# Picking the chosen pairs' expert numbers: thresholds and sums of index differences in place of a one-hot over 50 candidates

## The chip, the cores and the metric

The kernel runs on one core of one Trainium2 chip. The metric is the device time of one execution in microseconds (us). The engines are named PE (TensorE, matmul), DVE (VectorE), ACT (ScalarE), POOL (GpSimd) and SP (SyncE, which issues the transfers here).

## What is computed

Two transformer blocks, one after the other, on 256 tokens of width 1024. The first block ends in a PEER layer: each of 8 heads scores two sets of 128 keys, keeps the 16 best of each, adds them to 16 x 16 pair scores, keeps the 16 best pairs, and the pair's two key numbers name one of 128 x 128 experts. In the reference, cut to what matters here (`ub` and `vb` are the rows of `u` and `v` of the chosen experts, `gb` their gates):

```python
s = jnp.einsum('thpc,hpnc->thpn', q, subkeys).astype(jnp.float32)
s_top, i_top = lax.top_k(s, PEER_TOPK)
cand = s_top[:, :, 0, :, None] + s_top[:, :, 1, None, :]
cand_idx = i_top[:, :, 0, :, None] * PEER_N_KEYS + i_top[:, :, 1, None, :]
best, pos = lax.top_k(cand.reshape(T, PEER_HEADS, PEER_TOPK * PEER_TOPK), PEER_TOPK)
experts = jnp.take_along_axis(cand_idx.reshape(T, PEER_HEADS, PEER_TOPK * PEER_TOPK), pos, axis=-1)
gates = jax.nn.softmax(best, axis=-1).astype(h.dtype)
...
act = jax.nn.gelu(jnp.einsum('cd,ced->ce', xb, ub), approximate=False) * gb
return jnp.einsum('ce,ced->cd', act, vb)
```

The kernel doesn't gather: it computes all 16384 experts' products with the tokens and multiplies them by a gate that is zero for experts not chosen.

## The kernel before, in words

**Weights.** All large weights come as one stream of 128 x 128 blocks, 16 to a transfer (`raw`). `Stream.tile` splits eight blocks at a time into a high and a low part: `whi` is a copy by ACT (`L229`), `wlo` a difference (`L231`) that DVE makes for two tiles in three and POOL for the third (`W.pat = "DDP"`). Both have three buffers (`WB`), and `block` asks for one tile ahead of the one in use. Every product is three matmuls, lines 254 (high weights), 255 (high weights, low part of the tokens) and 256 (low weights).

**The stage around the change.** `both(uphase(0, 64), chain(topk(0), topk(1), topk_fin(0), topk_fin(1)), TKR)` (line 902) writes out the order by hand: after each weight tile of `uphase` (24 matmuls), the generator of the other side is advanced TKR times on average, up to its next `yield`. After every second tile ACT applies a GELU (`L198`, output `as`). `topk(tt)` treats 128 tokens: `top16` finds the 16 best of 128 scores for 16 half-heads (lines 809 to 813, one `yield` each); the sums of the 50 pairs that can be among the 16 best go to `cv` (DVE) and their expert numbers to `ce` (POOL) in seven steps (line 838); `top16` finds the 16 best of the 50 for each of 8 heads (`best`, `pos`, one `yield` each). Then the one-hot: for each head, `eq` (line 854, DVE) compares 16 positions with 50 numbers, `hit` (line 858, POOL) multiplies the result by `ce`, and `ex` (line 862, DVE) adds up over the 50. `eq` and `hit` have two buffers each. Casts, a shift and a mask (lines 869 to 873) make the two key numbers `f1` and `f2`. The softmax of `best` follows. `topk_fin` transposes `f1`, `f2` and the gate on PE (line 894) and copies them to float16 (`i1T`, `i2T`, `gT`).

`pace(r)` puts an instruction behind the last `wlo` that DVE had been given, so that the planner doesn't place it earlier.

**What follows.** `uphase(64, 96)` runs beside `gates(0)`, which builds one-hot matrices `p` and `eq` (lines 919, 921), the products `q` (924), multiplies them on PE (929) and scales the GELU's output `as` by the result (934), all but the matmul on DVE. Later stages: the products with `v`, a second block with convolution, delta rule, window attention and two feed-forward layers.

Of the kernel before, what the change touches and what calls it, by code (L numbers as in the profile page):

```python
# [23 lines left out]
F32 = mybir.dt.float32  # L24
F32R = mybir.dt.float32r
F16 = mybir.dt.float16
BF16 = mybir.dt.bfloat16
U32 = mybir.dt.uint32
AF = mybir.ActivationFunctionType
OP = mybir.AluOpType  # L30
AX = mybir.AxisListType
# [10 lines left out]
FF = 22  # L42
GB = 16
SPLIT_OUT1, SPLIT_XO, SPLIT_MIX, SPLIT_SWA = (3, 7), (3, 4, 6), (3, 4), (2, 5)
LAG, MIXR, TKR, DLR = 2, 1.15, 1.65, 4
EXPAT = "DDP"
NNOP = 0
PAT_QK, PAT_QKV = "DP", "DPP"
LB = 3, 3, 4, 3, 4, 2
# [17 lines left out]
def _consts():  # L67
    i = np.arange(128)
    f = np.float32
    out, at = {}, {}  # L70
    out["ident"] = np.eye(128, dtype=f)
    out["ones"] = np.ones((128, 128), f)
    out["bd64"] = (i[:, None] // 64 == i[None, :] // 64).astype(f)
    c1, out = out, {}
    out["negones"] = -np.ones((128, 128), f)
    out["negu"] = -(i[:, None] >= i[None, :]).astype(f)
    for n, mk in (("mbig", np.where(i[:, None] > i[None, :], f(BIG), f(0))),
                  ("mstr", np.where(i[:, None] >= i[None, :], f(-BIG), f(0)))):
        out[n] = np.concatenate([mk, np.zeros((128, 128), f), mk], 1)
    s4 = np.zeros((128, 4, 128), f)  # L80
    for h in range(4):
        s4[h, h, :] = 1
    out["sel4"] = s4.reshape(128, 512)
    o4 = np.zeros((128, 4, 4), f)
    for h in range(4):
        o4[:, h, h] = 1
    out["onec4"] = o4.reshape(128, 16)
    cm, out = out, c1
    out["eps"] = np.full((128, 1), EPS, f)
    out["iota"] = np.broadcast_to(i.astype(f)[None], (128, 128)).copy()  # L90
    c2 = {}
    hs = np.zeros((128, 2), f)
    hs[:64, 0] = 1
    hs[64:, 1] = 1
    c2["hsel"] = hs
    c2["tri"] = (i[:, None] <= i[None, :]).astype(f)
    c2["after"] = (i[:, None] > i[None, :]).astype(f)
    lv = []
    for s in (1, 2, 4, 8, 16, 32, 64):
        j, q = i[:, None], i[None, :]  # L100
        lv.append(((j // (2 * s) == q // (2 * s)) & ((q & s) > 0) & ((j & s) == 0)).astype(f))
    c2["lev"] = np.concatenate(lv, 1)
    q = np.arange(NMETA, T2)
    k = np.arange(T2)
    vis = (k[None] <= q[:, None]) & ((k[None] < NMETA) | (q[:, None] - k[None] < 128))
    msk = np.where(vis, f(0), f(-BIG)).astype(f)
    c2["msk0"] = msk[:128, :144]
    c2["msk1"] = msk[128:]
    mm = np.zeros((128, NMETA), f)
    mm[0, 15] = -BIG  # L110
    c2["mskm"] = mm

    def pack(d):
        at, o = {}, 0
        for n, a in d.items():
            at[n] = (o, a.shape[1])
            o += a.shape[1]
        return np.concatenate(list(d.values()), 1).astype(f), at

    a1, at1 = pack(c1)  # L120
    am, atm = pack(cm)
    a2, at2 = pack(c2)
    return a1, at1, am, atm, a2, at2
# [17 lines left out]
def tile_two_blocks(ctx, tc, ws, xT, memT, metaT, par_d, wsm_d, subk_d, c1_d, cm_d, c2_d, out, dumps=None):  # L141
    nc = tc.nc
    dumps = dumps or {}
    V, G, A, PE = nc.vector, nc.gpsimd, nc.scalar, nc.tensor

    def dump(name, ap, dst=None):
        if name in dumps:
            d = dumps[name]
            nc.sync.dma_start(d if dst is None else dst(d), ap)
# [23 lines left out]
    def C1(n, p=128):  # L173
        o, w = AT1[n]
        return c1[:p, o:o + w]
# [68 lines left out]
    W = Stream()  # L244
# [497 lines left out]
    with tc.tile_pool(name="pe", bufs=1) as mp:  # L742

        def asub():
            return mp.tile([128, 32, T1], F32, name="as", bufs=3)
# [4 lines left out]
        gT = mp.tile([128, 2, T1], F16, name="gT")  # L750
        iom = mp.tile([128, 128, 8], F16, name="iom")
        V.tensor_copy(iom, C1("iota").unsqueeze(2).to_broadcast([128, 128, 8]))
        iota = C1("iota")
        a0 = asub().rearrange("p a b -> p (a b)")
        subk = a0[:, :2048].rearrange("p (a b) -> p a b", a=16)
        nc.sync.dma_start(subk, subk_d)
# [45 lines left out]
        with tc.tile_pool(name="tk", bufs=1) as tp:  # L802
            def pace(r):

                after(r, W.last)
# [8 lines left out]
            PAIRS = [(a, 1, 16 // (a + 1)) for a in range(5)] + [(5, 3, 2), (8, 8, 1)]  # L814
            NCAND = 50

            fin = {}

            def topk(tt):
                top = tp.tile([128, 16, 16], F32, name="top")  # L820
                idx = tp.tile([128, 16, 16], U32, name="idx")
                for hp in range(16):
                    top16(top[:, hp], idx[:, hp], sc[:, tt, hp], 128)
                    yield
                idf = tp.tile([128, 16, 16], F32, name="idf")
                V.tensor_copy(idf, idx)
                tv = top.rearrange("p (h z) k -> p h z k", z=2)
                iv = idf.rearrange("p (h z) k -> p h z k", z=2)
                V.tensor_scalar(iv[:, :, 0], iv[:, :, 0], 128.0, None, op0=OP.mult)
                cv = tp.tile([128, 8, NCAND], F32, name="cv")  # L830
                ce = tp.tile([128, 8, NCAND], F32, name="ce")
                o = 0
                for a, na, nb in PAIRS:
                    for e, dst, src in ((V, cv, tv), (G, ce, iv)):
                        d = dst[:, :, o:o + na * nb].rearrange("p h (a b) -> p h a b", a=na)
                        x = src[:, :, 0, a:a + na].unsqueeze(3).to_broadcast([128, 8, na, nb])
                        y = src[:, :, 1, :nb].unsqueeze(2).to_broadcast([128, 8, na, nb])
                        e.tensor_add(d, x, y)
                    o += na * nb
                    yield  # L840
                best = tp.tile([128, 8, 16], F32, name="best")
                pos = tp.tile([128, 8, 16], U32, name="pos")
                for h in range(8):
                    top16(best[:, h], pos[:, h], cv[:, h], NCAND)
                    yield
                psf = tp.tile([128, 8, 16], F16, name="psf")
                V.tensor_copy(psf, pos)
                ex = tp.tile([128, 8, 16], F32, name="ex")
                W.pat = EXPAT
                hits = {}  # L850
                for h in range(9):
                    if h < 8:
                        eq = tp.tile([128, NCAND, 2, 8], F16, name="eq", bufs=2)
                        pace(V.tensor_tensor(eq, psf[:, h].rearrange("p (a b) -> p a b", a=2).unsqueeze(1).to_broadcast(
                            [128, NCAND, 2, 8]), iom[:, :NCAND].unsqueeze(2).to_broadcast([128, NCAND, 2, 8]),
                            op=OP.is_equal))
                        hits[h] = tp.tile([128, 16, NCAND], F32, name="hit", bufs=2)
                        G.tensor_mul(hits[h], eq.rearrange("p c a b -> p (a b) c"),
                                     ce[:, h].unsqueeze(1).to_broadcast([128, 16, NCAND]))
                        yield  # L860
                    if h:
                        pace(V.reduce_sum(ex[:, h - 1], hits.pop(h - 1), axis=AX.X))
                        yield
                W.pat = "DDP"
                eu = tp.tile([128, 128], U32, name="eu")
                i1 = tp.tile([128, 128], U32, name="i1")
                f1 = tp.tile([128, 128], F32, name="f1", bufs=2)
                f2 = tp.tile([128, 128], F32, name="f2", bufs=2)
                V.tensor_copy(eu, ex.rearrange("p h k -> p (h k)"))
                V.tensor_scalar(i1, eu, 7, None, op0=OP.logical_shift_right)  # L870
                V.tensor_copy(f1, i1)
                V.tensor_scalar(i1, eu, 127, None, op0=OP.bitwise_and)
                V.tensor_copy(f2, i1)
                dump("f1", f1, lambda d: d[tt])
                dump("f2", f2, lambda d: d[tt])
                yield
                g = tp.tile([128, 8, 16], F32, name="gt", bufs=2)
                V.tensor_sub(g, best, best[:, :, 0:1].to_broadcast([128, 8, 16]))
                act(g, g, AF.Exp)
                gs = tp.tile([128, 16], F32, name="gs")  # L880
                V.reduce_sum(gs[:, :8], g, axis=AX.X)
                V.reciprocal(gs[:, 8:], gs[:, :8])
                V.tensor_scalar(gs[:, 8:], gs[:, 8:], GSCALE, None, op0=OP.mult)
                V.tensor_mul(g, g, gs[:, 8:].unsqueeze(2).to_broadcast([128, 8, 16]))
                dump("gt", g, lambda d: d[tt].rearrange("p (a b) -> p a b", a=8))
                yield
                fin[tt] = f1, f2, g
# [16 lines left out]
        with tc.tile_pool(name="pg", bufs=1) as tp:  # L904
# [50 lines left out]
            for m in range(KC):  # L955
                V.scalar_tensor_tensor(X1[:, m], ys[m // 2][:, (m % 2) * T1:(m % 2 + 1) * T1], 1.0 / GSCALE, X1[:, m],
                                       op0=OP.mult, op1=OP.add)
# [3 lines left out]
    with tc.tile_pool(name="b2", bufs=1) as bp:  # L961
# [52 lines left out]
        with tc.tile_pool(name="m0", bufs=1) as mp:  # L1014
# [97 lines left out]
            for i, (t0, t1) in enumerate(TT2):  # L1112
                n = t1 - t0
# [226 lines left out]
        with tc.tile_pool(name="m1", bufs=1) as mp:  # L1340
# [197 lines left out]
            ge = early()  # L1538
# [119 lines left out]
```

## Time and profile before

| | us |
|---|---|
| median of 3 timed runs | 1960.94 |
| lowest and highest | 1957.55, 1965.3 |
| the profiled execution | 1955.38 |
| its span, from the first to the last instruction | 1953.7 |
| PE busy in the span | 1843.0 |
| DVE busy | 1361.0 |
| ACT busy | 864.5 |
| POOL busy | 628.8 |

The profile is one execution. A busy share is a mean over stages with different limits, so the stage that holds the change is to be read by itself: by stretches, by what PE waited for, and by the distance of events that mark equal amounts of its work. Durations in the trace are those of single instructions; where two engines wait for each other inside an instruction, the wait is part of its duration.

### The profile page before, as it was taken

To read this page: it belongs to the slowest core of one execution; us is meant where nothing else is said; L and a number is where in the kernel's file an instruction comes from. 1 tells how busy PE (TensorE), PEld (TensorE's weight loads), DVE (VectorE), ACT (ScalarE), POOL (GpSimd) and SP (SyncE) were. 2 spreads that over 40 slices of the span, in tenths; PEclk is the share of its full clock that TensorE was granted. 3 is DMA by queue.
4 is the path that set the end of the run, shared out by engine and by line. 5 is a ranking of instruction groups with operands and counts; after the bars stand their busy time and mean duration, and the time that the engine had idled before them with its cause. 6 is when DMAs were issued, how large, how long until landed. Compare 5 with 4: busy or idle time off the path is not lost.

```text
span 1953.7 us, 36962 instructions
## 1 busy us (share of the span) xinstructions
PE 1843.0 (94%) x15387; PEld 1772.1 (91%) x15387; DVE 1361.0 (70%) x2454; ACT 864.5 (44%) x1343; POOL 628.8 (32%) x384
## 2 busy tenths in 40 slices
PE   7999999989888899998899998899999999989999
PEld 6988999989888799998799998889999999679999
DVE  7746666898999965339974456864778845657872
ACT  5456554434432244443234444332444445644442
POOL 4312322373722222222222223332234422014442
PEclk9999999999999999999999998999999999989999
DMA  6432435535433355553345554211244443124453
GB/s 226 169 109 97 162 109 176 191 130 194 151 131 130 109 174 195 192 183 121 112 149 184 184 194 147 87 65 66 108 148 174 176 174 131 64 87 155 174 190 130
DMA packets 43128, 285.58 MB, mean 146 GB/s; under 512 B 5712, under 2 KB 8528, under 8 KB 9040
## 3 DMA queue, kind: packets, MB, share of 16 engines
q1 hardware_dynamic: 42960, 283.21, 40.7%
q8 instruction: 121, 1.98, 0.4%
q14 instruction: 47, 0.39, 0.1%
HBM read 282.14 MB, written 1.05 MB: 145 GB/s over the span
## 4 chain that ended last, share of the span: by engine, by line
PE 49%; DVE 19%; issue 3%; ACT 1%; POOL 0%; POOLq 0%; DVEq 0%; ACTq 0%
PE ps L254 9%; PE ps L255 9%; PE ps L256 9%; PE y L254 5%; PE y L256 5%; PE y L255 5%; DVE wlo L231 4%; DVE p L919 3%; DVE q L924 3%; DVE as L934 2%; DVE cy L973 2%; DVE eq L921 1%; PE pa L1443 1%; DVE hl L406 1%; DVE cy L971 1%
## 5 line engine op out<-in xcount | busy, mean ns | idle before, releaser
L229 ACT ACTIVATE whi<-raw 128x1024 fp32r<-128x1024 f32 x527 | 557.0, 1058 | 769.5 <-PE ps L255 500.5
L231 POOL TENSOR_TENSOR wlo<-raw,whi 128x1024 fp32r<-128x1024 f32 x180 | 455.6, 2531 | 955.9 <-ACT whi L229 939.7
L256 PE MATMUL ps<-xnh,wlo 128*128 128x256 f32 (+2 forms) x2336 | 677.5, 290 | 25.1 <-POOL wlo L231 15.9
L254 PE MATMUL ps<-xnh,whi 128*128 128x256 f32 (+2 forms) x2336 | 679.8, 291 | 14.1 <-ACT whi L225 6.9
L255 PE MATMUL ps<-xnl,whi 128*128 128x256 f32 (+2 forms) x2336 | 674.9, 289 | 0.8 <-DVE xnl L334 0.8
L231 DVE TENSOR_TENSOR wlo<-raw,whi 128x1024 fp32r<-128x1024 f32 x347 | 453.6, 1307 | 265.1 <-ACT whi L229 263.3
L256 PEld LDWEIGHTS ps<-xnh,wlo 128*128 128x128 f32 x2336 | 452.8, 194 | 31.8 <-POOL wlo L231 17.6
L254 PEld LDWEIGHTS ps<-xnh,whi 128*128 128x128 f32 x2336 | 453.5, 194 | 17.5 <-ACT whi L229 7.3
L255 PEld LDWEIGHTS ps<-xnl,whi 128*128 128x128 f32 x2336 | 451.9, 193 | 3.0 <-issue 1.6
L255 PE MATMUL y<-hl,whi 128*128 128x256 f32 x1024 | 289.8, 283 | 6.4 <-DVE hl L406 6.4
L254 PE MATMUL y<-hh,whi 128*128 128x256 f32 x1024 | 291.7, 285 | 0.5 <-ACT hh L405 0.5
L256 PE MATMUL y<-hh,wlo 128*128 128x256 f32 x1024 | 289.2, 282 | 3.2 <-DVE wlo L231 3.2
L255 PEld LDWEIGHTS y<-hl,whi 128*128 128x128 f32 x1024 | 195.6, 191 | 7.6 <-DVE hl L406 7.6
L256 PEld LDWEIGHTS y<-hh,wlo 128*128 128x128 f32 x1024 | 198.2, 194 | 4.0 <-DVE wlo L231 4.0
L254 PEld LDWEIGHTS y<-hh,whi 128*128 128x128 f32 x1024 | 195.6, 191 | 0.7 <-ACT hh L405 0.7
L406 DVE TENSOR_TENSOR hl<-as,hh 128x512 fp32r<-128x512 f32 x64 | 78.2, 1223 | 34.1 <-ACT hh L405 34.1
L254 PE MATMUL ps<-fh,whi 128*128 128x272 f32 (+1 forms) x352 | 100.1, 285 | 0.0
L256 PE MATMUL ps<-fh,wlo 128*128 128x272 f32 (+1 forms) x352 | 100.1, 284 | 0.0
L255 PE MATMUL ps<-fl,whi 128*128 128x272 f32 (+1 forms) x352 | 100.0, 284 | 0.0
L973 DVE SCALAR_TENSOR_TENSOR cy<-xpad,par,cy 128x272 f32<-128x272 f32 (+1 forms) x132 | 90.7, 695 | 2.6
L919 DVE TENSOR_TENSOR p<-iom,i1T 128x1024 f16<-128x1024 f16 x64 | 75.0, 1172 | 0.0
L929 PE MATMUL pa<-q,p 128*128 128x64 f16 x1024 | 43.5, 195 | 30.8 <-DVE as L934 25.2
(526 smaller groups left out, 2773.4 us busy)
## 6 DMA issues: line engine op xcount, KB each, us to landing
raw<-in_ws_dram SPq DMA_DIRECT2D x263, 1024.0 KB, 4.8
X<-in_xT_dram SPq DMA_DIRECT2D x4, 256.0 KB, 4.3
memX<-in_memT_dram SPq DMA_DIRECT2D x1, 1024.0 KB, 13.1
as<-in_subk_d_dram SPq DMA_DIRECT2D x1, 1024.0 KB, 6.9
out_dram<-X SPq DMA_DIRECT2D x4, 256.0 KB, 2.6
c<-in_c_d_dram SPq DMA_DIRECT2D x1, 793.0 KB, 4.3
cm<-in_cm_d_dram SPq DMA_DIRECT2D x1, 776.0 KB, 11.0
raw<-in_ws_dram SPq DMA_DIRECT2D x4, 128.0 KB, 4.1
```

The lines of the kernel that those rows point to most:

```text
L229: A.activation(hi, s, AF.Copy)
L231: r = e.tensor_sub(lo, s, hi.bitcast(F32))
L254: PE.matmul(ps, wh, xh, start=start, stop=False, **k)
L255: PE.matmul(ps, wh, xl, start=False, stop=False, **k)
L256: PE.matmul(ps, wl, xh, start=False, stop=stop, **k)
L406: V.tensor_sub(lo, x, hi.bitcast(F32))
L919: V.tensor_tensor(p1, index(0, 128), pairs(i1T, 128), op=OP.is_equal)
L921: V.tensor_tensor(eq, index(R * r, R), pairs(i2T, R), op=OP.is_equal)
L924: V.tensor_mul(q[:, z], eq, pairs(gT[:, z], R))
L929: PE.matmul(pg[:, t * R:(t + 1) * R], p1[:, a, :, b], q[:, z, a, :, b], start=z == 0, stop=z == 1)
L934: V.tensor_mul(a, a, pv[:, 32 * s:32 * s + 32])
L973: V.scalar_tensor_tensor(dst, xpad[:, j:j + T], P(wname, o + j), dst, op0=OP.mult, op1=OP.add)
```

## The change

The product with a one-hot over 50 candidates is replaced. The candidates lie in order of their first rank: rank 0 has 16, rank 1 has 8, and so on, so the first rank of a position follows from 16 thresholds, and the second is the position less the last threshold reached. `ge` compares the 16 positions of all 8 heads with the 16 thresholds in one instruction; the sum over ranks of `ge` times the step of the thresholds gives the last threshold reached; the sum of `ge` times the differences of neighbouring first key numbers (`d1`) gives the first key number; a comparison of the remaining rank with 0 to 15, times the second key numbers (`d2`), gives the second. All are float16, on DVE, over 128 x 2048 elements; the sums over 16 ranks are halved by additions (`fold`). `ce`, `hit`, `ex`, the cast to an integer, the shift and the mask go. Two constants of 16 columns are added. TKR goes from 1.65 to 1.5; EXPAT, equal to the pattern in use anyway, goes.

```diff
-LAG, MIXR, TKR, DLR = 2, 1.15, 1.65, 4
-EXPAT = "DDP"
+LAG, MIXR, TKR, DLR = 2, 1.15, 1.5, 4
...
+    thr = np.concatenate([[0], np.cumsum([16 // (a + 1) for a in range(15)])]).astype(f)
+    out["thr"] = np.broadcast_to(thr[None], (128, 16)).copy()
+    out["dthr"] = np.broadcast_to(np.diff(thr, prepend=f(0))[None], (128, 16)).copy()
...
+            thr, dthr, rank = (tp.tile([128, 16, 16], F16, name=n) for n in ("thr", "dthr", "rank"))
+            for t, c in ((thr, C1("thr")), (dthr, C1("dthr")), (rank, C1("iota")[:, :16])):
+                V.tensor_copy(t, c.unsqueeze(2).to_broadcast([128, 16, 16]))
...
-                idf = tp.tile([128, 16, 16], F32, name="idf")
-                V.tensor_copy(idf, idx)
+                iv = idx.rearrange("p (h z) k -> p h z k", z=2)
+                ix = tp.tile([128, 2, 8, 16], F16, name="ix")
+                V.tensor_copy(ix, iv.rearrange("p h z k -> p z h k"))
+                d1 = tp.tile([128, 8, 16, 2], F16, name="d1")
+                d2 = tp.tile([128, 8, 16, 2], F16, name="d2")
+                V.tensor_copy(d1[:, :, 0], ix[:, 0, :, :1].to_broadcast([128, 8, 2]))
+                for e in range(2):
+                    V.tensor_sub(d1[:, :, 1:, e], ix[:, 0, :, 1:], ix[:, 0, :, :15])
+                V.tensor_copy(d2, ix[:, 1].unsqueeze(3).to_broadcast([128, 8, 16, 2]))
+                yield
...
-                    for e, dst, src in ((V, cv, tv), (G, ce, iv)):
...
-                ex = tp.tile([128, 8, 16], F32, name="ex")
-                W.pat = EXPAT
-                hits = {}
-                for h in range(9):
-                    if h < 8:
-                        eq = tp.tile([128, NCAND, 2, 8], F16, name="eq", bufs=2)
-                        pace(V.tensor_tensor(eq, psf[:, h].rearrange("p (a b) -> p a b", a=2).unsqueeze(1).to_broadcast(
-                            [128, NCAND, 2, 8]), iom[:, :NCAND].unsqueeze(2).to_broadcast([128, NCAND, 2, 8]),
-                            op=OP.is_equal))
-                        hits[h] = tp.tile([128, 16, NCAND], F32, name="hit", bufs=2)
-                        G.tensor_mul(hits[h], eq.rearrange("p c a b -> p (a b) c"),
-                                     ce[:, h].unsqueeze(1).to_broadcast([128, 16, NCAND]))
-                        yield
-                    if h:
-                        pace(V.reduce_sum(ex[:, h - 1], hits.pop(h - 1), axis=AX.X))
-                        yield
...
+                def weighted(x, mask, d):
+
+                    pace(V.tensor_mul(x.rearrange("p h j (s e) -> p (h j) s e", e=2),
+                                      mask.rearrange("p h j (s e) -> p (h j) s e", e=2),
+                                      d.rearrange("p h j e -> p (h j) e").unsqueeze(2).to_broadcast([128, 128, 8, 2])))
+
+                def fold(x, out):
+
+                    n = 8
+                    while n > 1:
+                        V.tensor_add(x[:, :, :n], x[:, :, :n], x[:, :, n:2 * n])
+                        n //= 2
+                        if n == 4:
+                            yield
+                    V.tensor_add(out, x[:, :, 0], x[:, :, 1])
+                    yield
+
+                ge, x = cells("ge"), cells("gx")
+                pace(V.tensor_tensor(ge, slots16(psf), over_h(thr), op=OP.is_ge))
+                yield
+                pace(V.tensor_mul(x, ge, over_h(dthr)))
+                yield
+                rb_ = tp.tile([128, 8, 16], F16, name="rb_")
+                yield from fold(x, rb_)
+                V.tensor_sub(rb_, psf, rb_)
+                weighted(x, ge, d1)
+                yield
+                yield from fold(x, f1.rearrange("p (h k) -> p h k", h=8))
+                pace(V.tensor_tensor(ge, slots16(rb_), over_h(rank), op=OP.is_equal))
+                yield
+                weighted(x, ge, d2)
+                yield
+                yield from fold(x, f2.rearrange("p (h k) -> p h k", h=8))
```

## Rows read from the trace of the kernel before

**Rows 1.** The page, part 1: busy us, share of the span, instructions.

```profile
PE 1843.0 (94%) x15387; PEld 1772.1 (91%) x15387; DVE 1361.0 (70%) x2454; ACT 864.5 (44%) x1343; POOL 628.8 (32%) x384
```

**Rows 2.** Stretches: length, PE, PEld, DVE, ACT, POOL busy, granted clock, DMA, GB/s.

```profile
410.00:415.00 5.00, 3.23 (x26) 2.90 (x24) 5.00 (x5) 2.41 (x3) 4.07 (x2) 1.00 0.00 0
...
425.00:430.00 5.00, 0.48 (x2) 0.48 (x3) 5.00 (x3) 1.07 (x2) 4.47 (x2) 0.89 0.02 8
...
510.00:515.00 5.00, 1.68 (x8) 1.69 (x9) 5.00 (x4) 0.00 (x0) 4.43 (x2) 0.59 0.16 26
```

**Rows 3.** What PE waited for from 345 to 545: us, times, longest.

```profile
PE ps L256 <- POOL wlo L231: 12.8, 4, 5.4
```

**Rows 4.** ACT in order of time: start, us, what, idle before.

```profile
398.50 1.06 ACT L229 ACTIVATE whi<-raw 128x1024 fp32r<-128x1024 f32 x1 [1.83 <-PE ps L255]
...
404.13 1.06 ACT L229 ACTIVATE whi<-raw 128x1024 fp32r<-128x1024 f32 x1 [1.78 <-PE ps L255]
...
410.78 0.58 ACT L198 ACTIVATE as<-ps 128x512 f32<-128x512 f32 x1
...
418.89 1.06 ACT L229 ACTIVATE whi<-raw 128x1024 fp32r<-128x1024 f32 x1 [4.69 <-PE ps L255]
419.86 0.58 ACT L198 ACTIVATE as<-ps 128x512 f32<-128x512 f32 x1
...
425.49 0.58 ACT L198 ACTIVATE as<-ps 128x512 f32<-128x512 f32 x1
...
437.37 0.58 ACT L198 ACTIVATE as<-ps 128x512 f32<-128x512 f32 x1
...
505.53 0.58 ACT L198 ACTIVATE as<-ps 128x512 f32<-128x512 f32 x1
...
519.06 0.58 ACT L198 ACTIVATE as<-ps 128x512 f32<-128x512 f32 x1
```

**Rows 5.** POOL in order of time.

```profile
399.64 2.44 POOL L231 TENSOR_TENSOR wlo<-raw,whi 128x1024 fp32r<-128x1024 f32 x1 [6.11 <-ACT whi L229]
402.86 3.35 POOL L858 TENSOR_TENSOR hit<-eq,ce 128x800 f32<-128x800 f16 x1 [0.77 <-DVE eq L854]
...
423.86 2.32 POOL L858 TENSOR_TENSOR hit<-eq,ce 128x800 f32<-128x800 f16 x1 [0.58 <-DVE eq L854]
426.13 3.34 POOL L231 TENSOR_TENSOR wlo<-raw,whi 128x1024 fp32r<-128x1024 f32 x1
```

**Rows 6.** Tiles `eq` and `p`: shortest, median, longest in ns, times of the first and last.

```profile
L924 DVE TENSOR_TENSOR q<-eq,gT x128: 398/415/2577, 545.1 to 997.9; 128x512 f16<-128x512 f16 x128
...
L854 DVE TENSOR_TENSOR eq<-psf,iom x16: 562/1943/2820, 402.2 to 524.9; 128x800 f16<-128x800 f16 x16
...
L919 DVE TENSOR_TENSOR p<-iom,i1T x64: 1042/1074/3195, 541.5 to 993.4; 128x1024 f16<-128x1024 f16 x64
```

**Rows 7.** DVE in order of time.

```profile
396.71 1.23 DVE L231 TENSOR_TENSOR wlo<-raw,whi 128x1024 fp32r<-128x1024 f32 x1 [0.44 <-ACT whi L229]
...
403.83 2.82 DVE L854 TENSOR_TENSOR eq<-psf,iom 128x800 f16<-128x800 f16 x1
```

**Rows 8.** DVE's groups from 345 to 545: busy us, mean ns, idle before.

```profile
L854 DVE TENSOR_TENSOR eq<-psf,iom 128x800 f16<-128x800 f16 x16 | 27.9, 1750 | 0.1
L862 DVE TENSOR_REDUCE ex<-hit 128x16 f32<-128x800 f32 x16 | 15.6, 975 | 3.1 <-POOL hit L858 3.1
...
L869 DVE CAST eu<-ex 128x128 uint32<-128x128 f32 x2 | 2.8, 1388 | 0.1
...
L847 DVE CAST psf<-pos 128x128 f16<-128x128 uint32 x2 | 2.6, 1323 | 0.0
```

**Rows 9.** PE in order of time: the transposes of `topk_fin`.

```profile
538.26 0.38 PE L894 MATMUL pa<-c,f 128*128 128x128 f32 x2
```

**Rows 10.** What PE waited for from 545 to 706: us, times, longest.

```profile
PE pa L929 <- DVE as L934: 18.5, 11, 4.1
```

More of the change, by code (lines that the diff above doesn't have):

```diff
@@ L752, in tile_two_blocks @@
         V.tensor_copy(iom, C1("iota").unsqueeze(2).to_broadcast([128, 128, 8]))
-        iota = C1("iota")
         a0 = asub().rearrange("p a b -> p (a b)")
@@ L824, in topk @@
                     yield
-                idf = tp.tile([128, 16, 16], F32, name="idf")
-                V.tensor_copy(idf, idx)
+                iv = idx.rearrange("p (h z) k -> p h z k", z=2)
[8 more added lines that the diff above has]
+                yield
                 tv = top.rearrange("p (h z) k -> p h z k", z=2)
-                iv = idf.rearrange("p (h z) k -> p h z k", z=2)
-                V.tensor_scalar(iv[:, :, 0], iv[:, :, 0], 128.0, None, op0=OP.mult)
                 cv = tp.tile([128, 8, NCAND], F32, name="cv")
-                ce = tp.tile([128, 8, NCAND], F32, name="ce")
                 o = 0
                 for a, na, nb in PAIRS:
-                    for e, dst, src in ((V, cv, tv), (G, ce, iv)):
[L835 to L838, printed above, removed]
+                    V.tensor_add(cv[:, :, o:o + na * nb].rearrange("p h (a b) -> p h a b", a=na),
+                                 tv[:, :, 0, a:a + na].unsqueeze(3).to_broadcast([128, 8, na, nb]),
+                                 tv[:, :, 1, :nb].unsqueeze(2).to_broadcast([128, 8, na, nb]))
                     o += na * nb
@@ L864, in topk @@
-                W.pat = "DDP"
-                eu = tp.tile([128, 128], U32, name="eu")
-                i1 = tp.tile([128, 128], U32, name="i1")
                 f1 = tp.tile([128, 128], F32, name="f1", bufs=2)
                 f2 = tp.tile([128, 128], F32, name="f2", bufs=2)
[L869 to L872, printed above, removed]
@@ L873, in topk, with cells, over_h, slots16 @@
-                V.tensor_copy(f2, i1)
+                def cells(name):
+                    return tp.tile([128, 8, 16, 16], F16, name=name)
+                def over_h(c):
+                    return c.unsqueeze(1).to_broadcast([128, 8, 16, 16])
+                def slots16(x):
+                    return x.unsqueeze(2).to_broadcast([128, 8, 16, 16])
+                def weighted(x, mask, d):
+                    pace(V.tensor_mul(x.rearrange("p h j (s e) -> p (h j) s e", e=2),
+                                      mask.rearrange("p h j (s e) -> p (h j) s e", e=2),
+                                      d.rearrange("p h j e -> p (h j) e").unsqueeze(2).to_broadcast([128, 128, 8, 2])))
```

## The prediction

> **What bounds the kernel now.** I read the page's busy shares first: TensorE (PE) is busy for 94% of the span and VectorE (DVE) for 70% [rows 1], so a change on DVE counts only where PE waits for DVE or for something queued behind it. The changed lines lie in the stage that runs `uphase(0, 64)` beside `topk`, from about 347 to 543 us. Cut into stretches of 5 us, this stage has PE full nearly everywhere; the worst of the exceptions are 410-415, 425-430 and 510-515, in which the present one-hot runs and PE is busy for 3.23, 0.48 and 1.68 of 5 us [rows 2]. The waits of PE in the stage say on whom: 12.8 us in 4 waits, all of them for a `wlo` tile that GpSimd (POOL) makes, the longest 5.4 us [rows 3]. DVE is not named, though it is full there.
>
> What the stage loses is read best from the GELU that ends every second weight tile (`L198`). Two tiles take 5.65 us where nothing is amiss (419.86 to 425.49, and `whi` from 398.50 to 404.13, are 5.63). Three intervals are longer: 410.78 to 419.86 is 9.08, 425.49 to 437.37 is 11.88, 505.53 to 519.06 is 13.53 [rows 4]. Less 5.65 each, 3.4 + 6.2 + 7.9 = **17.5 us** are lost. That is more than the waits, since the granted clock falls with the long ones (0.59 of full speed in 510-515 [rows 2], so part of it at the lower level, 1.2 GHz, after PE had stood still).
>
> The cause is POOL's queue. Every third tile is POOL's; the one whose `whi` was copied at 418.89 gets its `wlo` only from 426.13, behind the `hit` of 423.86 (2.32 us), which itself had to wait for an `eq` [rows 4, 5]. An undisturbed `wlo` on POOL takes 2.44; this one took 3.34 [rows 5]. DVE suffers in turn: an `eq` of 0.56 us at its shortest took 2.82 from 403.83, and POOL's `hit` ran from 402.86 for 3.35, to 406.21 [rows 5 to 7]. So two-input work on the two engines waits for each other.
>
> The Trainium skill, SBUF — State Buffer, § "SBUF: two separate sides", calls this an exclusive lock: a DVE instruction with two SBUF inputs and a GpSimd instruction exclude each other, and the first to start keeps the pair to its end. The rows agree (2.82 beside 0.56). The rule speaks against the change as well as for it, since the new products are two-input too and will meet POOL's `wlo`; by it each meeting costs one whole instruction. The same figure comes out of the rows below.
>
> **Removed.** On POOL, 16 `hit` (2.32 and 3.35 us in the two rows shown, [rows 5]) and 14 short `ce` sums; POOL keeps only its `wlo`. On DVE, 16 `eq` (27.9 us), 16 `ex` (15.6) and the cast `eu` (2.8): 46.3 us in the stage, half per `topk` [rows 8]. The shorter casts beside them are left out. PE's three losses are all on a `wlo` behind a `hit`; with POOL's queue free, the 17.5 us should go. How much margin a POOL `wlo` then has: `whi` at 398.50 feeds the `wlo` at 399.64, which ends at 402.08; the buffers turn over every third tile, so that the tile is wanted when the `whi` two further on may start, at 404.13 [rows 4, 5]. That leaves 2.05 us. A DVE `wlo` takes 1.23 [rows 7], 1.2 less, so it has 3.3.
>
> **Added.** Per `topk` five float16 instructions of 2048 elements (`is_ge`, a product, two weighted products, `is_equal`), three folds of 1024 + 512 + 256 additions and a last one of 128, and one difference. None is in the trace. The nearest rows are `q` (512 elements, 0.398 at its shortest, pairs broadcast as in `weighted`) and `eq` (800, 0.562) [rows 6]: (0.562 - 0.398) / 288 = 0.57 ns per element and 0.106 fixed. So 1.27, 0.69, 0.40 and 0.25 for 2048, 1024, 512 and 256, and I take 0.25 for the last sum. Sum: 5 x 1.27 + 3 x 1.59 + 0.18 = 11.3 us per `topk`, 22.6 in all against 46.3. From above, `p` (1024 elements, strided, 1.042 [rows 6]) gives 1.98 for 2048, and float32 `wlo` (1024 in 1.23 [rows 7]) gives 2.3. I take the low end, as the new operands are dense or paired like those of `eq` and `q`. Below that nothing in the trace goes.
>
> The Trainium skill, VectorE: DVE Perf Modes, § "The perf-mode tier table", gives 1224 ns for a 16-bit two-tensor operation of 2048 elements and 2293 for a float32 one. By its figure the products would sum to 6.1 instead of 6.4 us, an estimate from that page; no run here shows it yet.
>
> **Does DVE keep up?** The section has 11 yields per `topk`, and TKR 1.5 hands out 4.5 per three tiles, so it lasts 7.3 tiles. Three tiles of PE are 1.5 x 5.65 = 8.5 us. DVE needs 4.5 x 11.3/11 = 4.6, two `wlo` of 1.23, and, at worst, one whole POOL `wlo` of 2.44 spent waiting: 9.5. The excess of 1.0 grows to 2.4 us over 7.3 tiles, below the 3.3 of margin: no stall. POOL's `wlo` waits for at most one DVE product, 1.27, below its 2.05. So the cost is 0 at best; I put **2 us** in for unlucky orders, and the upper end stands with the rivals.
>
> **The hand-over.** Before, `topk` has 49 yields, with the two `topk_fin` 100 in all, and at 1.65 per tile both `topk_fin` fall behind tile 61: their transposes stand together behind that tile, the first at 538.26 [rows 9]. After, it has 45 yields, 92 in all, and at 1.5 the last falls behind tile 62 (61 x 1.5 = 91.5). The `gates` behind it are bound by DVE (PE waits 18.5 us for `as` there [rows 10]), so a start one tile later costs between 0, if DVE does its `wlo` meanwhile, and 2.8. I take **1.5**.
>
> **Edits with one answer.** Index copies, differences and their pairs (`ix`, `d1`, `d2`; five short instructions, at most the 0.415 of a 512-element `q` each [rows 6], some 2 us per `topk`) are hidden by PE's full queue and by TKR: the 16-key part hands out 1.5 yields per tile for 1.65, which gives a tenth of its time back. Without that cover it is 4 us; a cast like `psf`, 1.32 on average [rows 8] for a size that needs far less, can also meet a POOL `wlo`. Three constant copies fall before the first `topk` step, ahead of the first `max`, and have the margin of a `wlo` as cover; uncovered they cost 1. The constants grow by 32 columns, on a transfer at the start that is long over. EXPAT equalled the other pattern, so its removal is nothing. The sum: -17.5 + 2 + 1.5 = **-14 us**. The profiled execution (1955.38 us, span 1953.7) would come to 1941.4; the three timed runs lie higher, at 1957.55 to 1965.3, and from their median of 1960.94 the forecast is **1947 us**.
>
> **Rivals.** *Half the gain:* the new products run at the pace of `p`. Then a `topk` needs 5 x 1.98 + 3 x 2.2 + 0.18 = 16.7 us, 6.8 per three tiles, 11.7 with `wlo` and one meeting, 3.2 too much; over 7.3 tiles 7.8, less the margin 4.5 of stall, 9 for both. -17.5 + 9 + 1.5 = -7: 1954. For it: the strided `p` row, and that no addition in float16 is shown. Against: `q` and `eq`.
>
> *Slower:* they run at the pace of float32 `wlo`: 19.1 us per `topk`, 1.74 per yield, 12.7 per three tiles, 10.2 too much, 6.9 of stall, 14 for both; a 2.3 us product holds POOL's `wlo` beyond its 2.05 (1.5 in all); two long stalls bring the clock down again (6.2 lost at 425 us where PE stood 4.5 [rows 2, 4], so 1.7 each, 3.4); the hand-over costs 2.8. Together 21.7 against 17.5: +4, 1965. It decides from about 1.7 us per yield. Against it: float16 instructions of both kinds of operand are faster in every row of theirs that met no one.
>
> *Absorbed:* DVE, full from 545 on, sets the end of `gates`, and an earlier PE only waits longer: 1961. Against: DVE's part of `gates` starts from `topk_fin`, whose transposes PE does between its tiles [rows 9], so DVE's start moves with PE.
>
> **How the numbers follow.** Forecast 0.62 (1943 to 1951 by its terms, some microseconds more by the spread of the runs), half the gain 0.22, absorbed 0.06, slower 0.10. The range of 8 in 10 goes from 1940 to 1961. A measurement of this kernel can tell about 0.5%, 9.8 us, from no change. Faster by more: 0.62; within: 0.31 (half, absorbed, and a slow rival that stays small); slower by more: 0.07.
>
> **What would show it.** Right: the three long GELU intervals fall to about 5.7; PE's waits for POOL's `wlo` in the stage fall below 3 us; products of 2048 elements take 1.2 to 1.3 us where POOL is idle and up to 3.7 where it isn't; the `gates` stretch keeps its length. Wrong: products near 2 us, PE waits for DVE's `wlo` in the new section, or a `gates` stretch longer by what the stage gained.

## The result, and the profile after

| | before | after |
|---|---|---|
| median of the timed runs, us | 1959.24 (4 runs) | 1941.64 (4 runs) |
| lowest and highest | 1957.28, 1965.30 | 1937.70, 1945.23 |
| ratio with 95% interval | | 0.9887 (0.9852 to 0.9922) |
| profiled execution, its span | 1955.38, 1953.7 | 1937.70, 1936.0 |

By that ratio the changed kernel is 1.1% faster. On the 1960.94 us that the prediction started from, the ratio is 1938.8 us (1931.9 to 1945.6 over the interval): the sign and the place were forecast, the size was not. 1947 lies above the interval, and 1938.8 lies 1.2 below the low end of 1940. The quotient of the two medians shown is 0.9910 (17.6 us); it lies inside the interval too, so that a few microseconds are within what these runs can tell. From profile to profile the span fell by 17.7 us.

The page's first part for the changed kernel answers to [rows 1] (busy us, share of the span, instructions):

```profile
PE 1844.8 (95%) x15387; PEld 1773.0 (92%) x15387; DVE 1335.9 (69%) x2457; ACT 865.8 (45%) x1343; POOL 574.9 (30%) x354
```

DVE is busy for 25.1 us less and POOL for 53.9 less, while PE is busy as before: it has less idle time. The three stretches of [rows 2], in the changed kernel (length, PE, PEld, DVE, ACT, POOL busy, granted clock, DMA share, GB/s):

```profile
410.00:415.00 5.00, 5.00 (x45) 5.00 (x44) 4.93 (x4) 2.61 (x3) 1.72 (x1) 1.00 0.45 138
425.00:430.00 5.00, 5.00 (x45) 5.00 (x44) 4.90 (x5) 3.25 (x5) 3.38 (x1) 1.00 0.59 205
510.00:515.00 5.00, 5.00 (x45) 5.00 (x44) 4.93 (x4) 3.27 (x4) 3.38 (x1) 1.00 0.50 200
```

PE is full in all three (3.23, 0.48 and 1.68 before) and its granted clock is 1.00. What PE waited for from 345 to 545, as in [rows 3]:

```profile
PE pa L957 <- DVE as L962: 1.4, 1, 1.4
PE ps L259 <- DVE wlo L234: 0.2, 1, 0.2
```

The 12.8 us on POOL's `wlo` are gone; what is left lies behind the stage, beside the start of `gates(0)`. The GELUs in order of time (start, duration, instruction) answer to [rows 4]:

```profile
411.02 0.58 ACT L201 ACTIVATE as<-ps 128x512 f32<-128x512 f32 x1
...
416.75 0.58 ACT L201 ACTIVATE as<-ps 128x512 f32<-128x512 f32 x1
...
422.38 0.58 ACT L201 ACTIVATE as<-ps 128x512 f32<-128x512 f32 x1
...
428.06 0.58 ACT L201 ACTIVATE as<-ps 128x512 f32<-128x512 f32 x1
```

The intervals are 5.73, 5.63 and 5.68 where they were up to 11.88. From the first GELU of `uphase` to the 32nd, the whole stage, it took 194.51 us before and 176.72 after: 17.8 less. I call this distance **the stage** below.

### The profile page after: what moved, and what is told of

Same layout as the page of the kernel before. It is cut to its first block, busy times and chain, and to the rows that moved or that the text cites. A ratio compares the mean times of both kernels' runs of the same rounds, so it can differ in the third digit from the quotient of the medians.

```text
span 1936.0 us, 36924 instructions
## 1 busy us (share of the span) xinstructions
PE 1844.8 (95%) x15387; PEld 1773.0 (92%) x15387; DVE 1335.9 (69%) x2457; ACT 865.8 (45%) x1343; POOL 574.9 (30%) x354
## 4 chain that ended last, share of the span: by engine, by line
PE 63%; DVE 18%; issue 3%; ACT 1%; POOL 0%; POOLq 0%; ACTq 0%; DVEq 0%
PE ps L257 14%; PE ps L258 14%; PE ps L259 14%; PE y L258 5%; PE y L259 5%; PE y L257 5%; DVE wlo L234 4%; DVE p L947 3%; DVE q L952 3%; DVE as L962 2%; DVE eq L949 2%; DVE cy L1001 1%; PE pa L1471 1%; DVE hl L409 1%; PE pa L1280 1%
## 5 line engine op out<-in xcount | busy, mean ns | idle before, releaser
L257 PE MATMUL ps<-xnh,whi 128*128 128x256 f32 (+2 forms) x2336 | 680.6, 292 | 12.7 <-ACT whi L228 7.2
L234 DVE TENSOR_TENSOR wlo<-raw,whi 128x1024 fp32r<-128x1024 f32 x347 | 441.2, 1272 | 269.7 <-ACT whi L232 267.9
L1001 DVE SCALAR_TENSOR_TENSOR cy<-xpad,par,cy 128x272 f32<-128x272 f32 (+1 forms) x132 | 85.2, 654 | 2.6
L947 DVE TENSOR_TENSOR p<-iom,i1T 128x1024 f16<-128x1024 f16 x64 | 70.2, 1097 | 0.0
```

What stands on the lines that cost most here:

```text
L234: r = e.tensor_sub(lo, s, hi.bitcast(F32))
L257: PE.matmul(ps, wh, xh, start=start, stop=False, **k)
L947: V.tensor_tensor(p1, index(0, 128), pairs(i1T, 128), op=OP.is_equal)
L1001: V.scalar_tensor_tensor(dst, xpad[:, j:j + T], P(wname, o + j), dst, op0=OP.mult, op1=OP.add)
```

## The experiments

Each run below is read by three numbers of its trace: the stage, the time from the 32nd to the 48th GELU (**the gates**: `uphase(64, 96)`, which runs beside `gates(0)`), and what PE waited for in the stage. Ratios are against the kernel before, run beside it.

| kernel | stage | gates | PE's waits in the stage (us, times) | ratio, or the time of a single run |
|---|---|---|---|---|
| before | 194.51 | 143.24 | POOL `wlo` 12.8 (4), DVE `wlo` 0.2 (1) | 1 |
| after | 176.72 | 143.74 | none | 0.9887 |
| again | 176.72 | 143.33 | none | 0.9895 |
| pad32 | 196.28 | 141.80 | POOL `wlo` 12.7 (3), DVE `wlo` 0.2 (1) | 0.9994 |
| expat_d | 190.49 | 142.79 | DVE `wlo` 9.7 (13) | 0.9998 |
| hit_dve | 196.97 | 142.69 | DVE `wlo` 14.8 (9) | 1974.29 us |
| pool_load | 197.72 | 143.53 | POOL `wlo` 12.3 (4), DVE `wlo` 3.4 (2) | 1.0038 |
| twice | 189.87 | 144.75 | DVE `wlo` 9.1 (4) | 1946.35 us |
| sec_d | 176.72 | 143.33 | none | 1928.98 us |
| tkr165 | 183.71 | 136.94 | DVE `wlo` 4.6 (3) | 1952.92 us |
| gates_d | 176.72 | 126.98 | none | 0.9821 |
| gates_d2 | 176.72 | 127.05 | none | 0.9773 |

The four runs with a time in the last column were timed once. Single times of one kernel lie too far apart (below) to say anything here, so these four are read by their traces alone.

**again: how large the gain is.** The changed kernel, unaltered, in more runs.

> The changed kernel once more, in five rounds. Theory A (the 17.5 us that the stage lost to POOL's queue are the whole gain, no part of it comes from elsewhere): ratio 0.990 to 0.992, so 15 to 19 us, and in the profile GELUs 5.63 to 5.73 us apart in the whole stage. Theory B (the change also gains some 5 us behind the stage, as the first pair of profiles shows between 1003 and 1180 us): ratio 0.987 to 0.989, and the matmuls of the product with v stand as close together as in the first profile of the changed kernel, 179 in 20 us against 172 before.

Measured: 1940.13 us in the median of 8 runs (1936.78 to 1951.88) against 1961.46 of 31 (1949.34 to 1979.11); ratio 0.9895 (0.9859 to 0.9932). The two comparisons agree, and by this one the gain is between 0.7 and 1.4%. 0.9895 lies between the two theories, and its interval covers both. In the trace the GELUs stand 5.63 to 5.73 us apart but for the last two intervals (5.94 and 6.01), and the matmuls of the product with `v` as close as in the first profile of the changed kernel, 179 in 20 us; whether the change does that, the next run says. Single executions of one kernel lie up to 30 us apart, so that a median of three or four can be off by several.

**pad32: is it the place of the tiles?** The kernel before with 32 unused columns of constants, as many as the change adds.

```diff
     out["iota"] = np.broadcast_to(i.astype(f)[None], (128, 128)).copy()
+    out["spare"] = np.zeros((128, 32), f)
```

> The kernel before with 32 unused columns added to the constants, nothing else, so that every tile behind them lies where the longer constants put it. Theory A: ratio 1.000 within 0.002, three long GELU intervals as before. Theory B (the place of the tiles in SBUF gives the closer matmuls of the product with v): ratio 0.996 to 0.998, and 179 matmuls in 20 us there.

Measured: 0.9994 (0.9959 to 1.0028), and the loss in the stage stays, on the same wait. Moved addresses and a longer load of constants don't explain the gain. The product with `v` has 179 matmuls in 20 us here too, as theory B said, but so has expat_d below, with neither the padding nor the change: it goes by the execution.

**expat_d: POOL without its `wlo` in the one-hot.** The kernel before, in which DVE makes all `wlo` while the one-hot runs; POOL keeps `hit`.

```diff
-EXPAT = "DDP"
+EXPAT = "D"
```

> The kernel before with all wlo of the one-hot's stretch made by DVE, none by POOL, so that no weight tile stands behind a hit in POOL's queue. If the queue is the cause: PE's 12.8 us of waits for POOL's wlo vanish, and only what DVE can't keep up with stays. DVE then needs per three tiles 5 yields of 46.3/34 = 1.4 us and three wlo of 1.2, some 10.5 us against 8.5, so that a part of the loss, 3 to 10 us, comes back as waits for DVE's wlo: ratio 0.995 to 0.999. If DVE's load is the cause and the queue only its messenger: the loss grows, ratio 1.002 or more.

What PE waited for in the stage:

```profile
PE ps L256 <- DVE wlo L231: 9.7, 13, 1.4
```

The waits for POOL's `wlo` are gone, as POOL has none to make there, but 13 short ones on DVE's come, the stage is only 4.0 us shorter, and the time is the same, 0.9998 (0.9963 to 1.0032). To take the `wlo` out of POOL's queue isn't enough while DVE has its part of the one-hot and all `wlo`. In the stage 13.8 of 17.8 us of loss are still there, more than the 3 to 10 that I had expected.

**hit_dve: POOL without `hit`.** The kernel before, with the product moved to DVE.

```diff
-                        G.tensor_mul(hits[h], eq.rearrange("p c a b -> p (a b) c"),
+                        V.tensor_mul(hits[h], eq.rearrange("p c a b -> p (a b) c"),
```

> The kernel before with the product hit on DVE instead of POOL: the old one-hot, POOL's queue free. If POOL's queue is the cause, PE's waits for POOL's wlo vanish, and what stays is DVE's load: per topk 8 x (0.56 + 0.94 + 0.98) = 19.8 us over 16 yields, 6.1 per three tiles, 11.0 with two wlo and one meeting against 8.5; over 9.7 tiles 8.1 too much, less the margin of 3.3: 4.8 per topk. Stage from the first to the 32nd GELU 182 to 188 us, against 194.5 and 196.3 before and 176.7 after. If the one-hot's form is the cause wherever it runs: 192 us or more.

The tile `hit` of this run (shortest, median, longest in ns, times of the first and the last):

```profile
L858 DVE TENSOR_TENSOR hit<-eq,ce x16: 1599/1750/3606, 406.0 to 531.2; 128x800 f32<-128x800 f16 x16
L862 DVE TENSOR_REDUCE ex<-hit x16: 965/980/994, 409.3 to 534.8; 128x16 f32<-128x800 f32 x16
```

The expectation was missed. PE's waits for POOL's `wlo` did vanish, but the stage is 196.97, no shorter than before and where I had put the other reading (192 or more), with DVE now late (14.8 us in 9 waits). I had priced `hit` at 0.94 us; on DVE it takes at least 1.60. It reads `eq` across (the 50 numbers of one position lie 16 elements apart) and multiplies by float32; which of the two costs the time, no run shows. Taken together with expat_d: to relieve POOL by giving DVE more does not bring the gain. What relief of DVE alone brings is the next run.

**pool_load: POOL's queue filled again.** The changed kernel with eight unused products on POOL per `topk` (128 x 800, as `hit` was, but shorter: 1.88 us in the median where `hit` took 2.64), each behind a small copy on DVE.

```diff
+                def load(h):
+                    junk = tp.tile([128, 16, NCAND], F32, name="junk")
+                    pk = tp.tile([128, 16], F16, name="pk", bufs=4)
+                    pace(V.tensor_copy(pk, psf[:, h]))
+                    G.tensor_mul(junk, pk.unsqueeze(2).to_broadcast([128, 16, NCAND]),
+                                 cv[:, h].unsqueeze(1).to_broadcast([128, 16, NCAND]))
...
                 pace(V.tensor_tensor(ge, slots16(psf), over_h(thr), op=OP.is_ge))
+                load(0)
```

> The changed kernel with eight products of 128x800 put back on POOL per topk, in the same section, their results unused, each behind a copy of 16 elements on DVE. If POOL's queue is the cause, the loss comes back though DVE does the new work: PE waits for POOL's wlo 6 to 15 us in the stage, GELU intervals of 8 us and more, ratio 0.993 to 0.999 against the kernel before. If the one-hot's load on DVE was the cause, the gain stays: ratio 0.987 to 0.991.

What PE waited for in the stage:

```profile
PE ps L259 <- POOL wlo L234: 12.3, 4, 3.5
PE ps L259 <- DVE wlo L234: 3.4, 2, 1.7
```

The whole gain is gone: 1.0038 (1.0000 to 1.0075), a stage of 197.72, and POOL's `wlo` is again what PE waits for, for nearly as long as in [rows 3]. The time is a little above what I expected (0.993 to 0.999). That work in POOL's queue is enough to hold PE is shown by this run: nothing else of the change was undone, and DVE does the new work. The stage is 3.2 us longer than before, though, with shorter products on POOL, and PE also waits 3.4 us for DVE's `wlo`. I put that down to the eight copies and to meetings with the load (a meeting is a two-input instruction of DVE and an instruction of POOL that fall together, so that one waits for the other); it wasn't tested by itself. Nor does the run part the queue from the meetings: the products on POOL brought both.

**twice: how much more DVE could bear.** The changed kernel with each of its five products of 2048 elements done twice, such as

```diff
-                pace(V.tensor_mul(x, ge, over_h(dthr)))
+                for _ in range(2):
+                    pace(V.tensor_mul(x, ge, over_h(dthr)))
```

> The changed kernel with each of the five products of 2048 elements done twice. By the margin reckoning of the prediction: 11.3 + 6.1 = 17.4 us per topk, 1.58 per yield, 7.1 per three tiles, 12.0 with wlo and a meeting, 3.5 too much; over 7.3 tiles 8.6, less the margin 5.3 of stall per topk: stage 184 to 190 us. If DVE has more room than reckoned (meetings cost less than a whole wlo): stage below 182.

Measured: the stage 189.87, within what the margins gave, and all of the loss on DVE:

```profile
PE ps L259 <- DVE wlo L234: 9.1, 4, 3.0
```

With five times 1.22 us more, a `topk` of 17.4 us in place of 11.3, 13.2 of the 17.8 us are lost again. The rival "half the gain" stood on a section of nearly this length (16.7 us, a loss of 9), so that the point it turned on is confirmed: the gain hung on the products' pace.

**sec_d: what the section costs by itself.** The changed kernel without a `wlo` on POOL in the new section. (In this expectation and in that of gates_d2 a window write is a `wlo` and a gate evaluation a GELU; the product beside the cast threshold is `gx<-ge,dthr`.)

```diff
                 ge, x = cells("ge"), cells("gx")
+                W.pat = "D"
...
+                W.pat = "DDP"
                 dump("f1", f1, lambda d: d[tt])
```

> The changed kernel with GpSimd given no window writes inside the new section alone (from the threshold comparison to the fold's last sum). Theory (the section costs VectorE what its instructions take undisturbed, the rest of their measured time is waiting for GpSimd's window writes): the weighted product beside the cast threshold takes 1.2-1.3 us where it took 3.3, the first fold sum 0.7 where it took 2.1 on average, no instruction of the section is over 1.5 us, and the stage from the first to the 32nd gate evaluation stays at 176-178 us, since TensorE had no wait there. Rival (the window writes that VectorE takes over cost it the same time again): a wait of TensorE on VectorE's window writes of 3 us or more appears and the stage is 180 us or longer.

The tile `gx` in the changed kernel, where POOL makes its `wlo`:

```profile
L879 DVE TENSOR_TENSOR gx<-gx x18: 286/424/2778, 412.8 to 515.1; 128x1024 f16<-128x1024 f16 x6, 128x512 f16<-128x512 f16 x6, 128x256 f16<-128x256 f16 x6
L871 DVE TENSOR_TENSOR gx<-ge,d x4: 1216/1218/1219, 416.9 to 510.6; 128x2048 f16<-128x2048 f16 x4
...
L889 DVE TENSOR_TENSOR gx<-ge,dthr x2: 3309/3309/3309, 409.5 to 494.7; 128x2048 f16<-128x2048 f16 x2
```

and in sec_d, where it makes none:

```profile
L879 DVE TENSOR_TENSOR gx<-gx x18: 291/418/693, 412.6 to 512.2; 128x1024 f16<-128x1024 f16 x6, 128x512 f16<-128x512 f16 x6, 128x256 f16<-128x256 f16 x6
L871 DVE TENSOR_TENSOR gx<-ge,d x4: 1217/1218/1220, 415.7 to 508.7; 128x2048 f16<-128x2048 f16 x4
...
L890 DVE TENSOR_TENSOR gx<-ge,dthr x2: 1220/1220/1220, 410.4 to 495.6; 128x2048 f16<-128x2048 f16 x2
```

The same product, 3.31 us beside a `wlo` of POOL and 1.22 without; the longest addition 2.78 and 0.69. The stage is 176.72 in both: what the meetings cost DVE was hidden.

**tkr165: the other constant.** The changed kernel with the old number of steps per weight tile.

```diff
-LAG, MIXR, TKR, DLR = 2, 1.15, 1.5, 4
+LAG, MIXR, TKR, DLR = 2, 1.15, 1.65, 4
```

> The changed kernel with TKR 1.65 as before. By the margin reckoning: 4.95 yields of 1.03 = 5.1, with wlo and a meeting 10.0, 1.5 too much per three tiles, over 6.7 tiles 3.3, the whole margin: stage 176.7 to 179. topk then ends some 6 tiles before the stage does; gates can begin its index products no earlier than the stage lets it, so that the distance from the 32nd to the 48th GELU stays 142 to 144, or is up to 3 us shorter if the products of its first tiles fill the time. If the new ratio carries part of the gain: 180 or more.

The stage was missed: 183.71, with 4.6 us of waits on DVE's `wlo`; by the stage alone the new ratio would carry part of the gain. But `gates(0)` starts earlier and the gates are shorter by 6.8; stage and gates together are 320.65, against 320.46 in the changed kernel and 337.75 before. What the edit to TKR moves is handed from one to the other, so that over the two together it has no part in the gain; the whole kernel was timed only once.

**gates_d and gates_d2: POOL's help where DVE is the bound.** PE waits in the gates for DVE, as before [rows 10] (the changed kernel, from 545 to 700):

```profile
PE pa L957 <- DVE as L962: 15.5, 8, 4.1
```

The meetings seen in the section happen there too, and there DVE, for which PE waits, has nothing to hide them behind. So in both `gates` stretches DVE was given all `wlo`; gates_d2 keeps it so over what lies between them, a product with `v` and `uphase(96, 128)`.

```diff
+            W.pat = "D"
             both(uphase(64, 96), gates(0), 1.1)
+            W.pat = "DDP"
             both(vphase(0, 32), none, 0)
             both(uphase(96, 128), none, 0)
+            W.pat = "D"
             both(vphase(32, 64), gates(1), 1.1)
+            W.pat = "DDP"
```

(gates_d; gates_d2 is without the two inner lines.)

> The changed kernel with all wlo made by DVE while the gates are built (both stretches), none by POOL. The runs so far say that a meeting with POOL's wlo costs DVE up to a whole wlo of 2.4 us, while a wlo given to POOL spares DVE 1.2. Where DVE is the bound, POOL's help would then cost more than it gives: from the 32nd to the 48th GELU the float16 instructions lose 26 us to meetings (p 1.12 to 1.20 on average against 1.05, q 0.54 to 0.60 against 0.41, eq 0.72 to 0.87 against 0.60), 11 more wlo cost 13. So that distance falls from 143.5 to 128 to 136, the second gates gains 3 to 8 more, ratio to the kernel before 0.980 to 0.985. If the meetings are not what it costs: 150 and more, ratio 0.992 or more.

> The changed kernel with all window writes on VectorE from the start of gates(0) to the end of gates(1), the v product between them included. Theory (the single 8.1 us wait that was left when only the two gates stretches were switched came from GpSimd's window write at 658 us, queued behind VectorE's gap-free stream): that write is then VectorE's own, no wait of TensorE over 4 us on a window write is left between 520 and 700 us, the stretch from the first to the 48th gate evaluation falls from 303.7 us to 294-298, and the time is about 1918 us (ratio to the kernel before about 0.978). Rival (VectorE's queue is long there anyhow, whoever writes): a wait of 5 us or more comes back on VectorE's window write, the stretch stays at 301-306 us and the time at 1926.

Measured: gates_d 1926.27 us, 0.9821 (0.9761 to 0.9882), the gates 126.98 in place of 143.74 (128 to 136 expected), although DVE makes half as many `wlo` again. DVE's `q` and `eq` of these stretches (busy us, mean ns, idle before), in the changed kernel from 525 to 690:

```profile
L952 DVE TENSOR_TENSOR q<-eq,gT 128x512 f16<-128x512 f16 x72 | 38.2, 566 | 0.0
...
L949 DVE TENSOR_TENSOR eq<-iom,i2T 128x512 f16<-128x512 f16 x38 | 32.7, 874 | 0.7
```

and in gates_d from 533 to 665:

```profile
L952 DVE TENSOR_TENSOR q<-eq,gT 128x512 f16<-128x512 f16 x67 | 27.9, 461 | 0.0
...
L949 DVE TENSOR_TENSOR eq<-iom,i2T 128x512 f16<-128x512 f16 x35 | 22.7, 653 | 0.0
```

`p` stayed at 1.11 to 1.12 on average, so it is `q` and `eq` that lost the meetings. gates_d2 measured 1912.67 us, 0.9773 (0.9731 to 0.9815), the best version here: 45 us, 2.3% less than before. One wait of PE had been left in gates_d between 640 and 700:

```profile
PE y L259 <- POOL wlo L234: 8.1, 1, 8.1
```

It isn't there in gates_d2. The number I had given for it, that stage and gates together fall to 294 to 298, was wrong (303.7 and 303.8, the rival's figure): the wait lies at 662 to 670, behind the 48th GELU. It shows where it should, in the start of the last `as` of the gates, at 971.0 in gates_d and 961.3 in gates_d2, 313.4 and 303.6 us behind the 48th GELU. In two traces of the changed kernel it was 311.7 and 315.0, so that the second gates' gain, too, appears in gates_d2 only. The two were timed beside different runs of the kernel before and their intervals overlap, so the times alone don't tell them apart.

## Why the prediction was right about the place and wrong about the size

- **What bounds, and the 17.5 us.** Right: 17.8 measured in the stage. The three long intervals went; of the stage's other intervals only the last two, 5.94 and 6.01, lie a little above 5.73. 176.72 comes back to the hundredth in four other traces. One slip of reading, of no weight: the view behind [rows 3] also has one wait of 0.2 us for a `wlo` of DVE.
- **POOL's queue as the cause.** Right, by pool_load. By expat_d and hit_dve it isn't enough to hand POOL's work to DVE while the one-hot is there.
- **Removed.** DVE -46.3 + 22.6 = -23.7 by the sum; -25.1 on the page, with the meetings in it on both sides. The sum sets busy time with waits in it against undisturbed time. An `eq` that met no one took 0.56 [rows 6], so 16 of them are 9.0 of the 27.9 us, and some 19 were waiting for POOL. Undisturbed, the old one-hot would need 8 x (0.56 + 0.97) = 12.3 us of DVE per `topk`, an estimate from these rows, and the new section needs 11.3: DVE was relieved mostly of its meetings with `hit`, and hardly of work.
- **The prices of the new instructions.** Right. Undisturbed in sec_d: 1.22 for 2048 elements (1.27 said), 0.69 for 1024 (0.69), 0.42 for 512 (0.40), 0.29 for 256 (0.25), 0.22 to 0.29 for the last sums (0.25). Five products are 6.1, three folds 4.2, the last sums and the difference 1.0: 11.3 us per `topk`, as worked out from `q` and `eq`. The figure of the Trainium skill, VectorE: DVE Perf Modes, § "The perf-mode tier table", 1224 ns (its column is bf16), agrees with the 1.22 measured here in float16, for a comparison and for products whose second operand is broadcast.
- **The meetings.** Right: the product of 3.31 us in the changed kernel began at 409.49 beside a `wlo` of POOL:

```profile
408.41 3.31 POOL L234 TENSOR_TENSOR wlo<-raw,whi 128x1024 fp32r<-128x1024 f32 x1 [6.13 <-ACT whi L232]
```

The POOL `wlo` came during `ge` (408.23, 1.23 long), waited 0.9 us for its end, ran its 2.40 to 411.72, and the product took 1.1 us more, to 412.80. Each waited until the other's instruction was over. That is the exclusive lock of the Trainium skill, SBUF — State Buffer, § "SBUF: two separate sides". Three meetings per `topk` cost DVE some 6 us (2.09 each), which the excess in the sum, one POOL `wlo` per three tiles, had in it.
- **The step that failed: +2 for new stalls, with the +1.5 below.** These are the mis-sized terms of the sum. The first measured 0. The sum said "no stall" (2.4 us behind, 3.3 of margin), and I added 2 for orders that I couldn't name. By `twice` the margin is used up by 6 us more per `topk`. From profile to profile 1941.4 was forecast and 1937.7 measured; of this miss of 3.7, 2 is this term, 1.0 the hand-over (0.5 for 1.5), 0.3 the stage (17.8 for 17.5), and 0.4 the chance named below.
- **The hand-over, +1.5.** It measured 0.1 to 0.5 in the gates (143.33 and 143.74 against 143.24). One tile later was right: the last transposes come 7.1 us ahead of the stage's end, where it was 9.9. But the transposes of the two `topk_fin` no longer stand together as in [rows 9]:

```profile
520.73 0.38 PE L922 MATMUL pa<-c,f 128*128 128x128 f32 x2
...
523.88 0.38 PE L922 MATMUL pa<-c,f 128*128 128x128 f32 x2
```

The first half of DVE's casts is done a tile before the second, and the last three intervals of the stage are 5.73, 5.94 and 6.01, where they were 6.17, 6.30 and 5.68. That this is why the hand-over cost so little wasn't tested.
- **The range.** Without the two terms the sum is 1960.94 - 17.5 = 1943.4, within the interval of the ratio (1931.9 to 1945.6). With its low end at 1940 the range left 3.4 us below that for the spread of the two medians, though the three times shown lay 8 us apart. So besides the two allowances, which pushed the forecast up, the range had too little room below for the measurement.
- **Absorbed.** Fell: DVE's part of the gates moved with the stage, its first `p` at 526.40 where it was at 541.52, 15.1 earlier, and the gates kept their length.
- **Slower.** Fell with the products' pace. `twice` at 1.58 us per yield lost 13.2 of 17.8; that the sign turns near 1.7 fits it and wasn't tried.

That the profiles differ by 17.7, as the stage does, is partly chance: in the traces the product with `v` behind the gates took 7.4 us less after, and the stretch from its end to the end of the span 6.7 more. Other runs of the same code show both without the change (below). The two ratios stand for 20.6 and 22.2 us of 1960.94, the two pairs of medians for 17.6 and 21.3; what lies between these and the stage's 17.8 is within the intervals, and whether any of it is the change isn't settled.

## What to carry to other kernels

An engine that helps with a shared stream (here POOL, every third `wlo`) can hold it up with any long work queued ahead of its share, so look for the helper's other work first, and count what it costs the engine it helps in meetings. New instructions were priced well here from the nearest rows of the same type and access, by a line through two sizes (and badly, in hit_dve, where the access was another), and the sum against a margin in time said whether they are hidden. Before you take a row's busy time as work removed, subtract what it waited. Where the working gives no stall, as here, put the doubt into the range and not into the sum, and widen the range by the spread of the medians.

## What the hardware showed beyond that

**POOL can be shut out for many instructions.** The one wait left in gates_d comes from a `wlo` of 2.40 us that took 12.56:

```profile
657.83 12.56 POOL L234 TENSOR_TENSOR wlo<-raw,whi 128x1024 fp32r<-128x1024 f32 x1 [136.60 <-ACT whi L232]
676.06 2.40 POOL L234 TENSOR_TENSOR wlo<-raw,whi 128x1024 fp32r<-128x1024 f32 x1 [5.67 <-ACT whi L232]
```

DVE's rows of that time in the same trace:

```profile
656.96 1.19 DVE L947 TENSOR_TENSOR p<-iom,i1T 128x1024 f16<-128x1024 f16 x1
657.95 0.86 DVE L952 TENSOR_TENSOR q<-eq,gT 128x512 f16<-128x512 f16 x2
...
666.91 0.81 DVE L409 TENSOR_TENSOR hl<-as,hh 128x512 fp32r<-128x512 f32 x1
667.51 0.72 DVE L949 TENSOR_TENSOR eq<-iom,i2T 128x512 f16<-128x512 f16 x1
678.67 1.22 DVE L234 TENSOR_TENSOR wlo<-raw,whi 128x1024 fp32r<-128x1024 f32 x1 [10.44 <-ACT whi L232]
```

POOL ended at 670.39, so its own 2.40 us began at 667.99, when DVE's unbroken run of two-input instructions, eighteen from 657.95 to 667.51, was at its end. In the section POOL got in after one instruction; in the changed kernel's gates, from 545 to 700, its `wlo` took up to 5.19 us. Each of these rows of DVE begins 0.2 us before the one ahead of it has ended. In the changed kernel's gates, from 559.57 to 582.65, it is at most 0.08, and several `q` end 0.03 before the next row begins; whether that is why POOL got no turn isn't settled.

**Two paces of TensorE at one clock.** In the product with `v` (50 us each; columns as above), the changed kernel and gates_d:

```profile
1042.00:1092.00 50.00, 50.00 (x444) 50.00 (x443) 26.51 (x22) 24.08 (x28) 15.45 (x7) 1.00 0.58 200
```

```profile
1027.00:1077.00 50.00, 50.00 (x427) 50.00 (x426) 25.49 (x21) 22.89 (x28) 14.43 (x6) 1.00 0.53 188
```

PE is full and its granted clock 1.00 in both, but it does 444 and 427 matmuls. The part from the last `as` of the gates to the last `hl` takes 169 to 170 us in nine of the traces and 175 to 177 in three: the kernel before, tkr165 and gates_d. The code there is the same, so it goes by the execution and not by the kernel; the cause stays open.

**The last part goes with the granted clock.** From the product's end to the end of the span the twelve traces took 762 to 779 us, again with the same code. The mean granted clock of that part was 0.97 in the five of 762 to 765 us (the kernel before among them), 0.96 in the six of 768 to 775 (the changed kernel's two among them), and 0.94 in the one of 779 (hit_dve). The 31 executions of the kernel before beside `again` show the same over the whole span: the shortest, 1949.34 us, had a mean granted clock of 0.973, the longest, 1979.11, one of 0.959. Why the clock differs between executions stays open.
